# Hyena's weight low parts computed in an earlier stage and kept in HBM, with a fourth load buffer in the hyena stage

## The chip, the cores and the metric

The kernel runs on one core of a Trainium2 chip. The core has five engines that each work through their own list of instructions in order: TensorE (PE, with weight loads shown apart as PEld), VectorE (DVE), ScalarE (ACT), GpSimd (POOL) and SyncE (SP). SP and POOL issue transfers; sixteen DMA engines carry them out. The metric is the device time of one execution in microseconds (us), as the median of several runs; lower is better.

## The reference

One token sequence of 256 rows and 1024 columns goes through three blocks, all in float32: a mixer of stick-breaking attention and memory attention followed by a feed-forward block with a squared relu, then latent attention (MLA) followed by a gated feed-forward block with a short convolution, then a hyena mixer followed by a second such feed-forward block. Every block ends in a layer norm of the scaled input plus the block's result. The two parts that the change touches are

```python
h = jnp.square(jax.nn.relu(x @ w_up[layer]))
x = layer_norm(DN_ALPHA * x + h @ w_down[layer], ...)
...
u = dwconv_centred(x @ w_in, w_short)
v, g1, g2 = jnp.split(u, 3, axis=-1)
z = v
for o, gate in enumerate((g1, g2)):
    k_f = jnp.fft.rfft(two_sided_kernel(filt[:, o, 0], filt[:, o, 1]), n=n, axis=0)
    y = jnp.fft.irfft(jnp.fft.rfft(z, n=n, axis=1) * k_f, n=n, axis=1)[:, :length]
    z = gate * (y + d_bias[o] * z)
return z @ w_o
```

The first is the squared-relu feed-forward (w_up is 1024 x 4096, w_down 4096 x 1024). The second is hyena: an input product with w_in (1024 x 3072), a convolution of width three, then two long convolutions, which the kernel does as products with cosine and sine matrices.

## The kernel before, in words

**Split products.** TensorE takes float32r, a rounded float32. To keep float32's precision every matrix is split into a high part, which is the value rounded by a copy, and a low part, which is the value minus the high part; a product is then three products: high by high, low by high and high by low. `split` (line 66) does it with one ACT copy and one DVE subtraction.

**Weights.** `weights` (line 74) brings a weight tile of 128 x 1024 (512 KB): SP loads it into one of three raw buffers (`wraw`), ACT writes the high part `whi` (line 67), and DVE the low part `wlo` (line 68). High and low parts have five slots each, so a tile's slot is free again when PE has used the tile five earlier. With `dma=True` the low part takes another way: ACT writes the negated high part into `wlo` (lines 84 and 85), and POOL's queue issues a second transfer of the same tile from HBM (high-bandwidth memory) that adds the weight to what lies there (line 86). DVE has no part in it. The raw buffer is free when both ACT copies are done.

**The squared-relu stage** has 32 steps. In step i PE multiplies the tile of w_up five steps ahead (`gemm_wide`, lines 110 to 112), ACT and DVE turn the result into h and split it (`ff1_act`, `act_split`), and PE multiplies the h of step i with a tile of w_down into four accumulator banks (lines 116 to 118). Each step takes two weight tiles. Besides, the rotation tables and the three layers of hyena's filter network are made there.

**The hyena stage** reads the x of the gated feed-forward block before it. Output tiles 0 to 3 of its input product come out of that block's end; tiles 4 to 23 are made by `hy_mm`, three times eight matmuls each into a PSUM bank `hin`. Tiles 0 to 7 are v, 8 to 15 g1 and 16 to 23 g2. `dwconv` runs the short convolution (one ACT pass, two DVE passes); for v and g1 PE then turns the tile over (`hyt`). `v_fin` splits v into `zh` and `zl`: `z0` is the first half of its columns (tiles 0 to 3), `z1` the second (tiles 4 to 7). `spectrum` multiplies z with the forward matrix (`X`) and, on DVE, with the filter's spectrum: four passes of up to 128 x 2048 into `spec_q` and `spec_w`. `even_odd` and `both` split the result into `yh` and `yl`, and `back1` and `back2` multiply that with the inverse matrix (`y`). The first long convolution runs through `back1` for both halves, the second through `back2`. In the end the result is multiplied with `hy_w_o`, eight tiles (`Down`, `acc`), the first four with `dma=True`.

The table `HY_DMA` says which of the tiles 4 to 23 take their low part by the accumulating transfer: eleven of them, 10, 12, 14 and 16 to 23. The main text of the stage (from `z0, z1 = new_z(), new_z()`) gives an order in which things are recorded; a scheduler then sets each engine's order by readiness and priority. `tc.issue_after(...)` keeps what is recorded in its scope behind a named instruction.

## Time and profile before

| | us |
|---|---|
| median of 3 runs | 965.1 (963.51 to 965.26) |
| the profiled execution | 964.65 |
| its span, first to last instruction | 962.9 |
| PE busy | 932.9 (97% of the span) |
| DVE busy | 761.1 (79%) |
| ACT busy | 539.9 (56%) |
| POOL busy | 64.0 (7%) |
| granted TensorE clock, mean | 0.992 |

The rows in fences are as the profile's views print them. A row of the trace in order of time has the start in us from the span's start, the duration, the engine, the line of the kernel, the operation and the tiles as out<-in, and in brackets how long the engine had stood idle before it and what ended that. "L68 DVE wlo<-wraw,whi" is line 68 on DVE writing `wlo` from `wraw` and `whi`. The granted clock is the share of full speed that TensorE was given. The DMA share is the mean busy share of the sixteen DMA engines.

### The profile page before, as it was taken

How to read it: one execution, taken by the hardware profiler on the slowest of the kernel's cores; microseconds unless marked ns; L12 is line 12 of the kernel's file. 1: busy time of each engine (PE TensorE's matmuls, PEld its weight loads, DVE VectorE, ACT ScalarE, POOL GpSimd, SP SyncE). 2: the span in 40 equal slices, each digit the busy share in tenths (PEclk: the TensorE clock that was granted, in tenths of full speed). 3: DMA queues.
4: the chain of work that ended last, by engine and by line, in shares of the span. 5: the costliest groups of instructions: out<-in, count | busy, mean ns of one | idle time of the engine just before them, and what ended most of it. 6: DMA issues, size and time to landing. Idle time of an engine off the chain costs nothing.

```text
span 962.9 us, 15208 instructions
## 1 busy us (share of the span) xinstructions
PE 932.9 (97%) x5808; PEld 823.7 (86%) x5808; DVE 761.1 (79%) x1201; ACT 539.9 (56%) x878; POOL 64.0 (7%) x61
## 2 busy tenths in 40 slices
PE   9999999999999999999999999998989999999996
PEld 6889788888887898788899999888978799999995
DVE  6887679777667879779889788889779878777776
ACT  4676636454445577556666566445675355555551
POOL 0000000000000010011312211001210000000000
PEclk9999999999999999999999999999989999999999
DMA  7764536655665443576555556436995565555551
GB/s 248 261 198 132 166 117 223 204 175 181 192 193 193 160 126 109 176 248 220 184 170 177 176 182 198 153 98 159 262 242 144 173 231 184 181 192 185 186 177 44
DMA packets 51082, 173.83 MB, mean 181 GB/s; under 512 B 6236, under 2 KB 7101, under 8 KB 50881
## 3 DMA queue, kind: packets, MB, share of 16 engines
q1 hardware_dynamic: 48656, 164.34, 52.6%
q0 software_dynamic: 2352, 8.52, 4.6%
q8 instruction: 46, 0.75, 0.3%
q14 instruction: 28, 0.22, 0.1%
HBM read 171.13 MB, written 1.05 MB: 179 GB/s over the span
## 4 chain that ended last, share of the span: by engine, by line
PE 75%; DVE 11%; DMA 7%; ACT 4%; issue 2%; SPq 0%; DVEq 0%; ACTq 0%; POOLq 0%
PE up L102 23%; PE acc L116 9%; PE acc L117 9%; PE acc L118 9%; PE up L110 5%; PE f L199 5%; DVE wlo L68 3%; PE up L112 3%; PE proj L102 2%; DMA wraw<-w_v 1%; ACT whi L67 1%; DMA wraw<-hy_w_in 1%; DMA wraw<-ffn_w_up_f 1%; PE hin L102 1%; DMA wraw<-w_qk 1%
## 5 line engine op out<-in xcount | busy, mean ns | idle before, releaser
L68 DVE TENSOR_TENSOR wlo<-wraw,whi 128x1024 fp32r<-128x1024 f32 (+1 forms) x255 | 310.4, 1220 | 78.4 <-ACT whi L67 77.5
L67 ACT ACTIVATE whi<-wraw 128x1024 fp32r<-128x1024 f32 (+1 forms) x255 | 265.2, 1044 | 128.1 <-PE acc L117 45.8
L102 PE MATMUL up<-x,whi 128*128 128x256 f32 x1280 | 173.7, 283 | 2.0 <-DVE t L790 2.0
L102 PEld LDWEIGHTS up<-x,whi 128*128 128x128 f32 x1280 | 164.8, 191 | 6.2 <-ACT whi L67 2.1
L118 PE MATMUL acc<-wlo,hh 128*128 128x512 f32 x304 | 119.9, 396 | 0.0
L116 PE MATMUL acc<-whi,hh 128*128 128x512 f32 x304 | 119.9, 396 | 0.0
L117 PE MATMUL acc<-whi,hl 128*128 128x512 f32 x304 | 119.9, 395 | 0.0
L102 PE MATMUL up<-x,wlo 128*128 128x256 f32 x640 | 89.8, 283 | 0.0
L787 ACT ACTIVATE t<-up,wc 128x256 f32<-128x256 f32 x80 | 37.7, 473 | 91.8 <-PE up L102 89.0
L102 PEld LDWEIGHTS up<-x,wlo 128*128 128x128 f32 x640 | 82.4, 192 | 0.0
L788 DVE SCALAR_TENSOR_TENSOR t<-up,wc,t 128x255 f32<-128x255 f32 x80 | 38.2, 479 | 46.3 <-ACT t L787 46.0
L118 PEld LDWEIGHTS acc<-wlo,hh 128*128 128x128 f32 x304 | 57.1, 188 | 13.5
L116 PEld LDWEIGHTS acc<-whi,hh 128*128 128x128 f32 x304 | 57.4, 189 | 11.3 <-ACT hh L67 0.5
L117 PEld LDWEIGHTS acc<-whi,hl 128*128 128x128 f32 x304 | 57.0, 188 | 11.0 <-DVE hl L68 0.3
L110 PE MATMUL up<-x,whi 128*128 128x512 f32 x224 | 56.6, 395 | 0.0
L165 POOL TENSOR_TENSOR ln_rs<-ln_rs,mhalf 128x1 f32<-128x1 f32 x12 | 11.5, 958 | 646.3 <-DVE ln_rs L164 646.3
L110 PEld LDWEIGHTS up<-x,whi 128*128 128x128 f32 x224 | 41.8, 188 | 10.6 <-issue 1.1
L102 PE MATMUL hin<-x,whi 128*128 128x256 f32 x320 | 46.7, 292 | 0.0
L102 PEld LDWEIGHTS hin<-x,whi 128*128 128x128 f32 x320 | 42.7, 199 | 0.3
L790 DVE SCALAR_TENSOR_TENSOR t<-up,wc,t 128x255 f32<-128x255 f32 x80 | 38.3, 480 | 2.1
L67 ACT ACTIVATE hh<-h 128x256 fp32r<-128x256 f32 x32 | 13.1, 415 | 39.1 <-DVE h L544 38.0
L112 PEld LDWEIGHTS up<-x,wlo 128*128 128x128 f32 x224 | 30.6, 190 | 2.3
(404 smaller groups left out, 1665.2 us busy)
## 6 DMA issues: line engine op xcount, KB each, us to landing
wraw<-ffn_w_up SPq DMA_DIRECT2D x80, 512.0 KB, 4.2
wraw<-ffn_w_down SPq DMA_DIRECT2D x44, 512.0 KB, 3.7
wraw<-w_down SPq DMA_DIRECT2D x32, 512.0 KB, 3.5
wraw<-w_up SPq DMA_DIRECT2D x28, 512.0 KB, 4.3
wraw<-hy_w_in SPq DMA_DIRECT2D x20, 512.0 KB, 5.1
wraw<-w_qk SPq DMA_DIRECT2D x14, 512.0 KB, 4.5
wlo<-hy_w_in POOLq DMA_DIRECT2D x11, 512.0 KB, 9.4
wraw<-w_out SPq DMA_DIRECT2D x8, 512.0 KB, 3.4
```

The costliest lines, as they stand in the source:

```text
L67: nc.scalar.activation(hi, src, AF.Copy)
L68: nc.vector.tensor_tensor(lo, src, hi.bitcast(F32), op=ALU.subtract)
L102: nc.tensor.matmul(ps, a[:, off + k * P:off + (k + 1) * P], m[:, k, :], start=i == 0, stop=i == len(seq) - 1)
L110: nc.tensor.matmul(ps, wh[:, k * P:(k + 1) * P], xx[:, k], start=k == 0, stop=False)
L112: nc.tensor.matmul(ps[:, :S], wl[:, k * P:(k + 1) * P], xh[:, k, :], start=False, stop=k == KT - 1)
L116: nc.tensor.matmul(ps, ah, mh, start=start, stop=False)
L117: nc.tensor.matmul(ps, al, mh, start=False, stop=False)
L118: nc.tensor.matmul(ps, ah, ml, start=False, stop=stop)
L199: nc.tensor.matmul(ps, x[xi][:, k, tb], ws[k // 2][wi][:, o:o + 512], start=i == 0, stop=i == len(seq) - 1)
L787: norm["act"] = nc.scalar.activation(dst, ps, AF.Copy, scale=w3[:, 1:2])
L788: nc.vector.scalar_tensor_tensor(dst[:, 1:], ps[:, :S - 1], w3[:, 0:1], dst[:, 1:], op0=ALU.mult, op1=ALU.add)
L790: norm["dve"] = nc.vector.scalar_tensor_tensor(dst[:, :S - 1], ps[:, 1:S], w3[:, 2:3], dst[:, :S - 1], op0=ALU.mult, op1=ALU.add)
```

## The change

1. **Low parts ahead of time.** `HY_DMA` shrinks to tiles 20, 21 and 22. For tiles 10 to 19 the low part is made in the squared-relu stage: at every second step from 1 to 21 `low_ahead` has POOL write a small mark that depends on the h made last, and behind it (for the first ten) issue a load of the next tile. Two steps later ACT and DVE split that tile in place, behind the split of the h made last by then, and POOL stores the low part to a tensor in HBM.
2. **Loading them.** In hyena those ten tiles take `low=`: ACT makes the high part alone, and SP loads the low part into its slot. Tile 23 goes back to the split by ACT and DVE.
3. **A fourth raw buffer.** During hyena every fourth `raw_tile` comes from a buffer in that stage's own pool. The room is found there by four buffers for `u` instead of six.
4. **z1 first.** z1's two `v_fin` now stand ahead of the first `spectrum` instead of among the products that follow it.
5. **hy_w_o's copies.** The tiles of `hy_w_o` that are accumulated by transfers are issued only after the first y part of `both`: their ACT copies and transfers are kept behind it.

```diff
-HY_DMA = (10, 12, 14, 16, 17, 18, 19, 20, 21, 22, 23)
+HY_AHEAD = range(10, 20)
+HY_DMA = (20, 21, 22)
...
     def raw_tile():
+        extra["n"] += 1
+        if extra["pool"] is not None and extra["n"] % (RAW_BUFS + 1) == 0:
+            return extra["pool"].tile([P, 1024], F32, name="wraw", tag="wraw_x")
         return wraw.tile([P, 1024], F32, name="wraw", tag="wraw")
...
+        if low is not None:
+            nc.scalar.activation(hi[:, :n], raw[:, :n], AF.Copy)
+            nc.sync.dma_start(lo[:, :n].bitcast(F32), low)
+            return hi, lo
...
+    ahead = {"todo": list(HY_AHEAD), "raw": None}
+
+    def low_ahead(act):
+        marks = [tc.issue_after(i.ins) for i in norm["split"]]
+        if ahead["raw"] is not None:
+            nt, raw = ahead["raw"]
+            hi = p2.tile([P, 1024], F32R, name="la_hi", tag="la_hi")
+            with marks[0], marks[1]:
+                split(hi, raw, raw)
+            lows[nt] = dram.tile([P, 1024], F32, name=f"low{nt}")
+            nc.gpsimd.dma_start(lows[nt], raw)
+            ahead["raw"] = None
+        if ahead["todo"]:
+            nt = ahead["todo"].pop(0)
+            raw = p2.tile([P, 1024], F32, name="la_raw", tag="la_raw", bufs=2)
+            mark = small.tile([P, 1], F32, name="mark", tag="mark")
+            done = nc.gpsimd.tensor_copy(mark, act[1][:, :1].bitcast(F32))
+            with tc.issue_after(done.ins):
+                nc.gpsimd.dma_start(raw, A["hy_w_in"][nt - 4])
+            ahead["raw"] = nt, raw
...
+        if i % 2 and i < 2 * len(HY_AHEAD) + 2:
+            low_ahead(ready[-1])
...
+    extra["pool"] = p4
...
-        w = weights(A["hy_w_in"][nt - 4], dma=nt in HY_DMA)
+        w = weights(A["hy_w_in"][nt - 4], dma=nt in HY_DMA, low=lows.get(nt))
...
-            u = p4.tile([P, S], F32, name="u", tag="u", bufs=6)
+            u = p4.tile([P, S], F32, name="u", tag="u", bufs=4)
...
-    s0 = spectrum(0, 0, z0, True)
-    v_fin(z1, 0, 4, va)
-    ga = pair_mm(8)
-    v_fin(z1, 1, 6, vb)
+    v_fin(z1, 0, 4, va)
+    v_fin(z1, 1, 6, vb)
+    s0 = spectrum(0, 0, z0, True)
+    ga = pair_mm(8)
...
+    yparts = norm["y"]
...
     for k in range(4):
-        dn.add((z0[0][:, k, :], z0[1][:, k, :]), A["hy_w_o"][k], True)
+        with tc.issue_after(yparts[0].ins):
+            dn.add((z0[0][:, k, :], z0[1][:, k, :]), A["hy_w_o"][k], True)
```

How instructions stand after scheduling, at three places (a number, the line, the operation with its tiles, and xN for N alike in a row). SP's list where hyena's weights are loaded; `hy_w_in` are its tiles from number 4 on, `hy_w_in_f` and `wc` belong to the stage's beginning and the one before. Before:

```order
170 L82 DMA wraw<-hy_w_in_f 128x1024 x3
171 L873 DMA wc<-ffn_w_conv 128x132
172 L82 DMA wraw<-hy_w_in_f 128x1024
173 L82 DMA wraw<-hy_w_in 128x1024 x20
174 L82 DMA wraw<-hy_w_o 128x1024 x8
```

The same place now; `low_1878` and the like are the stored low parts, from tile 10 on:

```order
173 L91 DMA wraw<-hy_w_in 128x1024 x8
174 L94 DMA wlo<-low_1878 128x1024
175 L91 DMA wraw<-hy_w_in 128x1024
176 L94 DMA wlo<-low_1985 128x1024
177 L91 DMA wraw<-hy_w_in 128x1024
178 L94 DMA wlo<-low_2117 128x1024
179 L91 DMA wraw<-hy_w_in 128x1024 x3
180 L94 DMA wlo<-low_2224 128x1024
181 L91 DMA wraw<-hy_w_in 128x1024
182 L94 DMA wlo<-low_2346 128x1024
```

The ten low loads stand among the raw loads in one list, so each waits for those ahead of it; on POOL's list eleven accumulating transfers of hyena's tiles have become three.

DVE's list around the first `spectrum` (its passes are `spec_w` and `spec_q`; `hyt_7019` before holds tiles 4 and 5 turned over, `hyt_7081` and `hyt_7096` now hold tiles 4 and 5, and 6 and 7). Before:

```order
737 L947 TENSOR_TENSOR zl<-hyt_6943,zh 128x2x256
738 L788 SCALAR_TENSOR_TENSOR u<-hin,ws,u 128x255
739 L68 TENSOR_TENSOR wlo<-wraw,whi 128x1024
740 L790 SCALAR_TENSOR_TENSOR u<-hin,ws,u 128x255
741 L68 TENSOR_TENSOR wlo<-wraw,whi 128x1024
742 L976 TENSOR_TENSOR spec_w<-ev,X_6995 128x512 x2
743 L976 TENSOR_TENSOR spec_w<-ev,X_7007 128x512 x2
744 L68 TENSOR_TENSOR zl<-hyt_7019,zh 128x2x256
745 L978 TENSOR_TENSOR spec_q<-spec_w,Kf 128x2048
746 L788 SCALAR_TENSOR_TENSOR u<-hin,ws,u 128x255
747 L979 TENSOR_TENSOR spec_q<-spec_q 128x2x512
748 L980 TENSOR_TENSOR spec_w<-spec_w,Kf 128x2048
```

And now:

```order
751 L986 TENSOR_TENSOR zl<-hyt_7035,zh 128x2x256
752 L828 SCALAR_TENSOR_TENSOR u<-hin,ws,u 128x255
753 L826 SCALAR_TENSOR_TENSOR u<-hin,ws,u 128x255 x2
754 L828 SCALAR_TENSOR_TENSOR u<-hin,ws,u 128x255
755 L71 TENSOR_TENSOR zl<-hyt_7081,zh 128x2x256
756 L828 SCALAR_TENSOR_TENSOR u<-hin,ws,u 128x255
757 L1015 TENSOR_TENSOR spec_w<-ev,X_7117 128x512 x2
758 L71 TENSOR_TENSOR zl<-hyt_7096,zh 128x2x256
759 L826 SCALAR_TENSOR_TENSOR u<-hin,ws,u 128x255
760 L1015 TENSOR_TENSOR spec_w<-ev,X_7129 128x512 x2
761 L828 SCALAR_TENSOR_TENSOR u<-hin,ws,u 128x255
762 L1017 TENSOR_TENSOR spec_q<-spec_w,Kf 128x2048
```

Both halves of z1 are now finished ahead of the long passes, and the two weight low parts that stood here (tiles 8 and 9) have moved up, ahead of z0's end.

ACT's list around the last but one y, that of the second convolution's first half (`yh`; `g_6820` and `g_6912` are g2, `zh<-u` the result of `back2`). Before:

```order
558 L85 ACTIVATE wlo<-wraw 128x1024
559 L787 ACTIVATE g_6820<-hin,ws 128x256
560 L84 ACTIVATE whi<-wraw 128x1024
561 L67 ACTIVATE yh<-spec_q 128x512 x2
562 L85 ACTIVATE wlo<-wraw 128x1024
563 L787 ACTIVATE g_6820<-hin,ws 128x256
564 L84 ACTIVATE whi<-wraw 128x1024
565 L67 ACTIVATE yh<-spec_w 128x512 x2
566 L787 ACTIVATE g_6820<-hin,ws 128x256
```

And now:

```order
561 L70 ACTIVATE yh<-spec_q 128x512 x2
562 L825 ACTIVATE g_6912<-hin,ws 128x256
563 L70 ACTIVATE yh<-spec_w 128x512 x2
564 L825 ACTIVATE g_6912<-hin,ws 128x256
565 L97 ACTIVATE whi<-wraw 128x1024
566 L98 ACTIVATE wlo<-wraw 128x1024
567 L97 ACTIVATE whi<-wraw 128x1024
568 L98 ACTIVATE wlo<-wraw 128x1024
569 L70 ACTIVATE zh<-u 128x256
570 L97 ACTIVATE whi<-wraw 128x1024
```

The copies of `hy_w_o` (whi by L97, wlo by L98) that stood among y's parts and before them now all stand behind them, and the third and fourth of them among the parts of `back2`.

More of the change, by code (lines that the diff above doesn't have):

```diff
@@ L50, in block_kernel @@
     wspl = ctx.enter_context(tc.tile_pool(name="wspl", bufs=SPLIT_BUFS))
+    dram = ctx.enter_context(tc.tile_pool(name="dram", bufs=1, space=bass.MemoryType.DRAM))
+    lows = {}
     lnp = ctx.enter_context(tc.tile_pool(name="lnp", bufs=1))
@@ L66, in split, with weights @@
     def split(hi, lo, src):
-        nc.scalar.activation(hi, src, AF.Copy)
-        nc.vector.tensor_tensor(lo, src, hi.bitcast(F32), op=ALU.subtract)
+        return (nc.scalar.activation(hi, src, AF.Copy),
+                nc.vector.tensor_tensor(lo, src, hi.bitcast(F32), op=ALU.subtract))
     norm = {"inst": None, "after": 0}
+    extra = {"pool": None, "n": 0}
     def raw_tile():
+        extra["n"] += 1
+        if extra["pool"] is not None and extra["n"] % (RAW_BUFS + 1) == 0:
+            return extra["pool"].tile([P, 1024], F32, name="wraw", tag="wraw_x")
         return wraw.tile([P, 1024], F32, name="wraw", tag="wraw")
-    def weights(ap, dst=None, dma=False):
+    def weights(ap, dst=None, dma=False, low=None):
         n = ap.shape[-1]
@@ L299, in act_split @@
         lo = pool.tile([P, S], F32R, name=tag + "l", tag=tag + "l", bufs=bufs)
-        split(hi, lo, ps)
+        norm["split"] = split(hi, lo, ps)
         return hi, lo
@@ L1011, in both @@
                 for j, t in enumerate((q, w)):
-                    split(y[0][:, i, j], y[1][:, i, j], t[:, i, 0])
+                    norm["y"] = split(y[0][:, i, j], y[1][:, i, j], t[:, i, 0])
         return y
@@ L1040, in back2 @@
                     n == 0, n == 3)
-            t = p4.tile([P, S], F32, name="u", tag="u", bufs=6)
+            t = p4.tile([P, S], F32, name="u", tag="u", bufs=4)
             nc.vector.tensor_tensor(t, ps[:, :S], g2[:, 4 * c + q, :], op=ALU.mult)
@@ L1092, in block_kernel @@
     x, utok = dn.end(gb, ALPHA_2, A["ffn_w_up_f"][1], [(room[:, i, 0], room[:, i, 1]) for i in range(4)])
+    extra["pool"] = None
     ph.close()
```

## The prediction

> **What bounds the kernel now.** I read the page first, then a table of stretches, then the rows in order of time around each wait of TensorE, and last the DMA queues of two stages.
>
> ```profile
> PE 932.9 (97%) x5808; PEld 823.7 (86%) x5808; DVE 761.1 (79%) x1201; ACT 539.9 (56%) x878; POOL 64.0 (7%) x61
> ```
>
> TensorE (PE) is busy 97% of the span, so all that an edit can win is its 30 us of idle time and what the clock withholds. The stretches that matter, in us from the span's start (columns: length, then busy time and count by engine, granted clock, DMA share, GB/s):
>
> ```profile
> 633.00:763.00 130.00, 120.66 (x788) 109.71 (x787) 110.70 (x164) 77.66 (x112) 14.11 (x16) 0.96 0.72 195
> 650.00:676.40 26.40, 22.37 (x166) 21.66 (x165) 23.43 (x34) 13.25 (x21) 2.68 (x3) 0.94 0.64 169
> 676.40:706.40 30.00, 25.56 (x177) 23.50 (x175) 21.08 (x31) 22.94 (x33) 6.07 (x7) 0.94 1.03 260
> 706.40:724.60 18.20, 18.20 (x119) 16.85 (x120) 16.03 (x22) 14.09 (x21) 4.37 (x5) 0.91 0.98 233
> 724.60:763.00 38.40, 37.52 (x205) 31.38 (x204) 35.02 (x54) 17.45 (x27) 0.99 (x1) 1.00 0.59 183
> 656.00:664.00 8.00, 5.44 (x33) 5.24 (x33) 7.30 (x10) 2.37 (x4) 0.88 (x1) 0.79 0.38 85
> 698.00:712.00 14.00, 10.01 (x39) 7.97 (x38) 7.71 (x15) 10.55 (x16) 2.62 (x3) 0.76 1.04 261
> 150.00:265.00 115.00, 115.00 (x571) 95.15 (x570) 86.24 (x151) 60.84 (x94) 0.00 (x0) 1.00 0.60 187
> 420.00:440.00 20.00, 18.18 (x140) 17.36 (x139) 17.18 (x27) 14.21 (x24) 4.39 (x3) 1.00 0.84 289
> ```
>
> Hyena's input product and convolutions fill 633 to 763. There PE idles 130.00 - 120.66 = 9.3 us, and its clock loses (1 - 0.79) x 8 = 1.7 us at 656 to 664 and (1 - 0.76) x 14 = 3.4 us at 698 to 712. Together 14.4 us: the ceiling of a gain in this stage. The squared-relu stage (150 to 265 of it) has PE at 115.00 of 115.00: nothing to win, only to lose. The rows of PE in hyena that waited long (start, duration, line, operation, and in brackets the idle time before it with its releaser):
>
> ```profile
> 659.14 0.50 PE L935 MATMUL hyt<-ident,u 128*128 128x128 f32 x2 [2.56 <-DVE u L790]
> ...
> 670.01 1.22 PE L102 MATMUL hin<-x,wlo 128*128 128x256 f32 x8 [1.47 <-DMA wlo<-hy_w_in]
> ...
> 700.10 1.54 PE L102 MATMUL hin<-x,wlo 128*128 128x256 f32 x8 [1.82 <-DMA wlo<-hy_w_in]
> ...
> 706.38 0.47 PE L116 MATMUL y<-yh,c_inv1h 128*128 128x512 f32 x1 [2.17 <-DVE g L790]
> ```
>
> Three causes: a convolution on DVE (VectorE) queued behind the spectrum's long products (2.56 us); low parts that an accumulating DMA of the POOL queue brings late (1.47, 1.82); and the y product at 706.38 (2.17), late because its inputs were. Those go back to ACT (ScalarE) and a raw load, in ACT's rows
>
> ```profile
> 699.67 1.06 ACT L85 ACTIVATE wlo<-wraw 128x1024 fp32r<-128x1024 f32 x1 [2.69 <-DMA wraw<-hy_w_in]
> ```
>
> and DVE's:
>
> ```profile
> 702.12 0.69 DVE L68 TENSOR_TENSOR yl<-spec_q,yh 128x512 fp32r<-128x512 f32 x1 [6.93 <-ACT yh L67]
> ```
>
> ACT stood 2.69 us for a raw tile, and DVE 6.93 us for the copies of y that ACT has behind it. The load was slow because the 16 DMA engines were full: share 1.03 in 676 to 706. By queue and by issue, 633 to 724 (q0 is POOL's, q1 SP's; the last figure is the median landing in us):
>
> ```profile
> q0 software_dynamic: 1919, 7.01, 40.7%
> q1 hardware_dynamic: 3024, 11.01, 36.5%
> ...
> wraw<-hy_w_in SPq DMA_DIRECT2D x16, 512.0 KB, 5.1
> wlo<-hy_w_in POOLq DMA_DIRECT2D x11, 512.0 KB, 9.4
> wraw<-hy_w_o SPq DMA_DIRECT2D x7, 512.0 KB, 8.4
> wlo<-hy_w_o POOLq DMA_DIRECT2D x4, 512.0 KB, 8.6
> ```
>
> 40.7% of 91 us is 37.0 us for 7.01 MB: 2.77 us of all 16 engines for an accumulation of 512 KB (0.524 MB). 36.5%, 33.2 us for 11.01 MB, makes 1.58 us for a plain load.
>
> **The change, part by part.** *Hyena's transfers.* Eight accumulations go (22.2 us of the engines), ten plain loads of low parts come (15.8 us): 70.2 us becomes 63.8. ACT loses eight negating copies (8 x 1.06, the 699.67 row, = 8.5 us), and a raw buffer is free again after one copy. A low load can start when the low slot of the tile five earlier has been read, five tiles of PE's work ahead of its use, and a tile is three times the eight matmuls of the 670.01 row (1.22), about 3 us with overlap; raw loads land in 5.1. I expect PE to wait for none. SP holds them in line with the raw loads, so a low load that waits for its slot holds up raw loads behind it, and the reverse; the fourth raw buffer covers that. Cover gone, each late tile costs like today's, 1.5 to 1.8 us.
>
> [...]
>
> *The first y product (stretch 650 to 676.4).* DVE's chain sets when it can start; two of its rows:
>
> ```profile
> 660.52 1.22 DVE L68 TENSOR_TENSOR wlo<-wraw,whi 128x1024 fp32r<-128x1024 f32 x1
> ...
> 669.70 1.29 DVE L68 TENSOR_TENSOR yl<-spec_w,yh 128x512 fp32r<-128x512 f32 x2
> ```
>
> Today y's last low part ends at 669.70 + 1.29 = 671.0, but PE, delayed, only comes at 676.4. The change takes tile 11's low part (1.22, the first row) off this chain, and puts the low parts of tiles 8 and 9 and z1's finish ahead of the spectrum, so that no transpose waits behind the long products: y's parts are there by about 669.8. PE, without its waits (26.40 - 22.37 = 4.0) and the half clock (1.7), comes at 670.7, 0.9 us after them. Gain 5.7; late next is this same chain.
>
> *The second (676.4 to 706.4).* Idle 30.00 - 25.56 = 4.4, and half of the 3.4 us of clock, 1.7: PE comes at 694.6 in the new time, 670.7 + 30.0 - 6.1. Without DVE's 6.93 us wait y's parts could be there that much before today's 706.4, at 699.5; shifted by 5.7 that is 693.8, 0.8 ahead of PE. Gain 6.1.
>
> *The third (706.4 to 724.6)* has no idle time, but the other 1.7 us of half clock, which follows the 2.17 us gap. Gain 1.7. Tile 23's low part comes back to DVE here (1.22), where DVE is busy 16.03 of 18.20; tiles 13 and 15 give as much back before. Convolution buffers fall from six to four: a convolution then waits for the transposes of the one four before, done a pair of tiles earlier, so nothing; with that cover gone, some tenths at each. Sum of the gains: 13.5 us.
>
> *hy_w_o's copies behind y's parts.* Four raw tiles are copied twice by ACT and accumulated into by POOL. Today the last of those DMAs is issued at 722.72 in POOL's rows,
>
> ```profile
> 722.72 0.88 POOL L86 DMA_DIRECT2D wlo<-hy_w_o  x1 [2.44 <-ACT wlo L85]
> ```
>
> before the second half's y product and 11 us before the first product with hy_w_o, in PE's rows:
>
> ```profile
> 724.57 0.28 PE L116 MATMUL y<-c_inv2h,yh 128*128 128x256 f32 x1
> ...
> 733.97 0.40 PE L116 MATMUL acc<-whi,zh 128*128 128x512 f32 x1
> ```
>
> Behind the change the first pair of copies (2.1 us) starts about when that y product does (724.57 here) and POOL issues 0.5 later; with a landing of 8.6 that is 11.2 us in. PE wants the low part 733.97 + 0.5 - 724.57 = 9.9 in. Late by 1.3 at the median landing, by 0 if the copies get ahead of the order that I read, by 2.1 at 9.4, the median of hyena's own tiles. I take 1.0, just under the nearest row's.
>
> *The squared-relu stage.* Ten times in about 115 us come a load and a store of 512 KB on POOL's queue, one more split on ACT and DVE, and a mark on POOL that holds the load back. The page's rows for such a split, the stage's DMA (150 to 305) and ACT's largest wait for a weight slot there:
>
> ```profile
> L68 DVE TENSOR_TENSOR wlo<-wraw,whi 128x1024 fp32r<-128x1024 f32 (+1 forms) x255 | 310.4, 1220 | 78.4 <-ACT whi L67 77.5
> L67 ACT ACTIVATE whi<-wraw 128x1024 fp32r<-128x1024 f32 (+1 forms) x255 | 265.2, 1044 | 128.1 <-PE acc L117 45.8
> ```
> ```profile
> q1 hardware_dynamic: 8615, 29.14, 60.1%
> ...
> wraw<-w_down SPq DMA_DIRECT2D x28, 512.0 KB, 3.4
> wraw<-w_up SPq DMA_DIRECT2D x22, 512.0 KB, 4.3
> ```
> ```profile
> ACT whi L67 <- PE up L110: 22.6, 21, 1.9
> ```
>
> DVE goes from 86.2 to 98.4 of 115 us, ACT from 60.8 to 71.2: both keep room. A transfer is 60.1% of 155 us over 29.14 MB, 1.68 us; twenty make 33.6, so the share rises from 0.60 to 0.89. A store from POOL's queue isn't in this trace; I price it as a load, and with 2.77, the accumulation's, as its dear end the share is 0.99. PE uses a weight tile every 2.82 us (571 matmuls in 115 us, 28 for two tiles). Three raw buffers, each taken for its landing, the two copies (1.04, 1.22) and some tenths, 2.6 us in all beside the landing, keep that pace up to a landing of 3 x 2.82 - 2.6 = 5.9 us. Medians are 3.4 and 4.3; a transfer of POOL's delays what it overlaps by about its own 1.68, so I estimate 5. ACT mostly waits for PE to free a slot (22.6 us), so weights stand ready. On POOL nothing but the layer norm's powers comes behind these transfers, eleven steps after the last. Price 0 to 6, taken 0.5 since the estimate is under the limit; below nothing is excluded, as PE is full there.
>
> *New short waits* at the y products, with 0.9 us of room at the first: 0 to 5, taken 1.0, near today's smallest (1.47).
>
> Net: 13.5 - 1.0 - 0.5 - 1.0 = 11.0 us. The profiled execution took 964.65 (span 962.9 and 1.75 around it), 0.45 below the median of the runs, 965.1. So 954.1, rounded to 954.0.
>
> **The rivals.** *The gaps move and the clock stays low.* DVE's chain is 2 us later than I sum at two of the y products. Gaps of about 1.3 us each return, and a half-clock stretch (1.7) follows one: 4.3 lost, 958.4. For it: DVE is busy 23.43 of 26.40. Against: it loses work there. [...]
>
> *The DMA engines stay the bound: no change.* If a low load among raw ones costs what an accumulation did, the stretches with a share near 1 stay as they are; only the 2.56 us gap goes with its half clock (4.3), less the 2.5 of costs and 0 to 3.2 for two more transfers: 963 to 966. Against: 1.58 against 2.77. [...]
>
> *Slower: the squared-relu stage starves.* hy_w_o's raw loads landed in 8.4 us where the engines were full. At 8.4 a raw buffer turns in 11.0 us, a tile each 3.67, 0.85 over the pace; 41 tiles make 35 us, less four split tiles of backlog (11.3): 23.5 lost, 977. It decides from a landing of about 7.5, where the loss (22.4 - 11.3 = 11.1) eats the net gain. For it: share 0.89 to 0.99. Against: 420 to 440 moves 289 GB/s at 0.84, and the mark paces POOL by PE's own progress. The case: 967 to 977.
>
> **How the numbers follow.** Forecast 0.63 (951 to 957), moved gaps 0.20 (957 to 962), DMA-bound 0.07 (963 to 966), starved 0.10 (967 to 977). A measurement of this kernel can tell about 0.2%, 1.9 us. Faster 0.63 + 0.20 = 0.83, same 0.07, slower 0.10. The low end, 950.5, is the whole ceiling of 14.4 us; the range up to 963 leaves out the last two cases and a little below.
>
> **What would show it.** Right: 150 to 265 with PE full, DMA share near 0.9, landings near 5; no wait of PE for hyena's low parts; clock 1.00 from 650 to 720; the first two y products near 671 and 695; a wait of about 1 us before the first products with hy_w_o. Wrong: PE waiting in the squared-relu stage, landings over 6 there, or y products where they stand today.

## The result, and the profile after

| | before | changed |
|---|---|---|
| median of 4 runs, us | 964.65 (963.51 to 965.26) | 956.53 (955.58 to 959.44) |
| ratio to before, 95% interval | | 0.9922 (0.9898 to 0.9946) |
| profiled execution: time, span | 964.65, 962.9 | 956.31, 954.0 |
| granted clock, mean | 0.992 | 0.997 |

The changed kernel is faster by 8.1 us in the medians and by 8.9 in the spans of the two profiled executions, where the net forecast was 11.0. A later set of twelve runs of the same kernel ("changed again" below) has a median of 959.7, at 0.9946 of the kernel before: 5 us faster. First the page's row for PE (TensorE), then the table of stretches of the changed kernel, columns as before the change:

```profile
PE 928.3 (97%) x5808; PEld 820.7 (86%) x5808; DVE 768.8 (81%) x1209; ACT 540.3 (57%) x880; POOL 72.6 (8%) x83
```
```profile
150.00:265.00 115.00, 115.00 (x572) 95.37 (x571) 95.08 (x159) 67.94 (x101) 13.17 (x29) 1.00 0.80 264
656.00:664.00 8.00, 8.00 (x67) 7.91 (x66) 7.76 (x8) 3.99 (x6) 0.00 (x0) 1.00 0.80 259
698.00:712.00 14.00, 14.00 (x108) 13.53 (x107) 13.70 (x16) 5.02 (x10) 0.00 (x0) 1.00 0.11 40
722.00:740.00 18.00, 14.09 (x64) 10.49 (x64) 14.43 (x15) 9.12 (x12) 0.86 (x1) 1.00 0.97 279
```

The squared-relu stage still has PE full (115.00 of 115.00). The two stretches that had PE idle and a clock of 0.79 and 0.76 are full at 1.00. From 698 to 712 the DMA engines are nearly idle (0.11); from 722 to 740 they are full (0.97), and PE has 3.9 us of idle time that was not there before. PE's rows show where:

```profile
672.34 0.48 PE L129 MATMUL y<-yh,c_inv1h 128*128 128x512 f32 x1
...
695.23 0.39 PE L129 MATMUL y<-yh,c_inv1h 128*128 128x512 f32 x1
...
712.62 0.35 PE L129 MATMUL y<-c_inv2h,yh 128*128 128x256 f32 x1 [0.23 <-DVE g L828]
...
722.05 0.39 PE L129 MATMUL acc<-whi,zh 128*128 128x512 f32 x1
...
724.34 0.50 PE L131 MATMUL acc<-wlo,zh 128*128 128x512 f32 x1 [1.66 <-DMA wlo<-hy_w_o]
...
728.13 0.50 PE L131 MATMUL acc<-wlo,zh 128*128 128x512 f32 x1 [0.73 <-DMA wlo<-hy_w_o]
...
731.98 0.50 PE L131 MATMUL acc<-wlo,zh 128*128 128x512 f32 x1 [0.78 <-DMA wlo<-hy_w_o]
...
735.79 0.51 PE L131 MATMUL acc<-wlo,zh 128*128 128x512 f32 x1 [0.74 <-DMA wlo<-hy_w_o]
...
738.23 0.28 PE L129 MATMUL y<-c_inv2h,yh 128*128 128x256 f32 x1
```

and, of the kernel before, the first y product and the one behind hy_w_o's four tiles:

```profile
676.44 0.48 PE L116 MATMUL y<-yh,c_inv1h 128*128 128x512 f32 x1
...
745.18 0.29 PE L116 MATMUL y<-c_inv2h,yh 128*128 128x256 f32 x1
```

The first two y products come at 672.3 and 695.2 (676.4 and 706.4 before), and no hyena product waits for a low part. But each of the first four tiles of hy_w_o waits for its own accumulated low part. From the first product with hy_w_o to the next y product it takes 738.23 - 722.05 = 16.2 us; before, 745.18 - 733.97 = 11.2. The 5.0 us lost are more than the 3.9 of idle time: the first product behind a gap takes 0.50 to 0.51 instead of 0.39 to 0.40, and its overlap with the one ahead of it (0.16: products otherwise start 0.23 to 0.24 apart) is gone.

To compare kernels I cut the way from the hyena stage's first transposes (f4t) to the next stage's first product (up) at the same products in each trace. This keeps out what happens ahead of f4t, which differs by up to 3.5 us between two executions of the same kernel (626.49 and 630.02 for the changed one). y1, y2 and y3 are the first products of the first three y in PE's rows. The products with X stand in other stretches from kernel to kernel (0.23 us each; 7 of them between y1 and y2 in the changed kernel, 12 in that with low parts ahead alone), so a single column is good to 1 or 2 us between kernels; the sums don't have this.

| kernel | f4t to y1 | y1 to y2 | y2 to y3 | y3 to hy_w_o | its four tiles | then to up | sum | ratio of times to before (95%) |
|---|---|---|---|---|---|---|---|---|
| before | 50.70 | 29.94 | 18.19 | 9.40 | 11.21 | 32.10 | 151.5 | |
| changed | 45.85 | 22.89 | 17.39 | 9.43 | 16.18 | 30.38 | 142.1 | 0.9922 (0.9898 to 0.9946) |
| changed again | 45.95 | 22.89 | 17.38 | 9.44 | 15.25 | 30.37 | 141.3 | 0.9946 (0.9923 to 0.9969) |
| no hold | 46.87 | 22.89 | 17.38 | 9.45 | 11.20 | 31.37 | 139.2 | 0.9906 (0.9882 to 0.9929) |
| no hold again | 45.84 | 22.89 | 17.38 | 9.44 | 11.20 | 31.34 | 138.1 | 0.9888 (0.9867 to 0.9910) |
| hy_w_o split plainly | 47.22 | 22.89 | 17.39 | 9.44 | 11.19 | 32.84 | 141.0 | 0.9914 (0.9898 to 0.9931) |
| three buffers | 48.08 | 23.16 | 16.06 | 10.16 | 16.60 | 33.55 | 147.6 | 0.9991 (0.9978 to 1.0005) |
| three buffers, no hold | 47.11 | 23.16 | 16.07 | 13.12 | 11.20 | 31.78 | 142.4 | 0.9952 (0.9933 to 0.9971) |
| z1 late | 45.57 | 23.57 | 16.95 | 9.25 | 16.52 | 30.38 | 142.2 | 0.9930 (0.9915 to 0.9946) |
| no low parts ahead | 50.02 | 30.10 | 15.14 | 10.13 | 16.19 | 31.59 | 153.2 | 0.9996 (0.9980 to 1.0011) |
| low parts ahead alone | 51.24 | 23.80 | 17.06 | 9.05 | 11.20 | 32.70 | 145.1 | 0.9965 (0.9944 to 0.9987) |
| low loads by POOL | 45.81 | 22.90 | 17.38 | 9.45 | 16.63 | 30.73 | 142.9 | 0.9940 (0.9915 to 0.9964) |
| hy_w_o ahead too | 45.77 | 22.89 | 17.38 | 9.44 | 11.20 | 30.93 | 137.6 | 0.9973 (0.9956 to 0.9990) |
| twice the traffic | 47.14 | 22.89 | 17.38 | 9.44 | 16.32 | 30.37 | 143.5 | 1.0150 (1.0127 to 1.0173) |

The column f4t to y1 needs a word. In the traces of four kernels (hy_w_o split plainly, three buffers with the hold, no low parts ahead, low parts ahead alone) a stretch at half clock (granted 0.50), worth 1.7 us, stands right behind f4t. The other traces have the same gap of 1.1 us there and no such stretch. I take it for a chance of the execution (last section); it is taken off below where I say so.

### The profile page after: what moved, and what is told of

Read it like the earlier page. It is cut to its first block, busy times and chain, and to the rows that moved or that the text cites. A ratio compares the mean times of both kernels' runs of the same rounds, so it can differ in the third digit from the quotient of the medians.

```text
span 954.0 us, 15307 instructions
## 1 busy us (share of the span) xinstructions
PE 928.3 (97%) x5808; PEld 820.7 (86%) x5808; DVE 768.8 (81%) x1209; ACT 540.3 (57%) x880; POOL 72.6 (8%) x83
## 4 chain that ended last, share of the span: by engine, by line
PE 81%; DVE 7%; DMA 6%; ACT 4%; issue 2%; DVEq 0%; SPq 0%; ACTq 0%
PE up L115 23%; PE acc L129 9%; PE acc L131 9%; PE acc L130 9%; PE up L123 5%; PE f L212 5%; PE hin L115 5%; PE up L125 3%; PE proj L115 2%; DVE wlo L71 2%; ACT whi L70 1%; DMA wlo<-hy_w_o 1%; DMA wraw<-w_qk 1%; DMA wraw<-w_v 1%; PE ln_t L191 1%
## 5 line engine op out<-in xcount | busy, mean ns | idle before, releaser
L70 ACT ACTIVATE whi<-wraw 128x1024 fp32r<-128x1024 f32 (+1 forms) x253 | 262.4, 1044 | 117.1 <-PE acc L130 46.1
L115 PE MATMUL hin<-x,whi 128*128 128x256 f32 x320 | 44.7, 286 | 0.0
L70 ACT ACTIVATE hh<-h 128x256 fp32r<-128x256 f32 x32 | 13.1, 413 | 36.9 <-DVE h L557 35.8
```

The costliest lines, as they stand in the source:

```text
L70: return (nc.scalar.activation(hi, src, AF.Copy), nc.vector.tensor_tensor(lo, src, hi.bitcast(F32), op=ALU.subtract))
L115: nc.tensor.matmul(ps, a[:, off + k * P:off + (k + 1) * P], m[:, k, :], start=i == 0, stop=i == len(seq) - 1)
```

## The experiments

**No hold (twice).** Part 5 undone:

```diff
-        with tc.issue_after(yparts[0].ins):
-            dn.add((z0[0][:, k, :], z0[1][:, k, :]), A["hy_w_o"][k], True)
+        dn.add((z0[0][:, k, :], z0[1][:, k, :]), A["hy_w_o"][k], True)
```

> Part 5 undone: hy_w_o's copies and accumulations are no longer kept behind y's parts; the rest is the changed kernel. In the changed kernel TensorE waits four times for hy_w_o's accumulated low parts (1.66, 0.73, 0.78 and 0.74 us, 3.9 in all; the four tiles of products take 16.2 us from first to next y product where they took 11.2 before: 5.0 lost). Theory: this is where the missing gain went. Undone, the four waits go, but eight copies of 1.04 us stand between 697 and 712, where ScalarE is busy about 11 of 17 us, so y's parts and the y product at 712.6 come 1 to 3 us later: 952.5 to 955, 1.5 to 4 below the changed kernel's 956.5. Rival A: the hold earns more than it costs; the copies push the y product back by 5 us or more: 957 or above. Rival B: the waits for hy_w_o are due to the engines being full in that stretch (DMA share 0.96 in 724 to 740) whenever the copies are made; then they stay near 3.9 and the time is 956 to 957.

> Part 5 undone once more, on the chip of the next three, so that the medians can be set side by side. Theory: from the hyena stage's first transposes (f4t) to the next stage's first product it takes 139 to 140 us, against 141.3 and 142.1 in the two profiles of the changed kernel and 151.5 before; the first product with hy_w_o follows the y product by 9.4 us and the four tiles take 11.2: a ratio of 0.989 to 0.992 to the kernel before. Rival: the first profile was lucky, the waits for hy_w_o's low parts come back in part: 142 and a ratio above 0.992.

Measured: 955.53 us (952.95 to 960.44) and 955.27 (952.13 to 958.45). POOL's rows show the four accumulations, first in the changed kernel, then without the hold:

```profile
715.21 0.86 POOL L99 DMA_DIRECT2D wlo<-hy_w_o  x1 [24.77 <-ACT wlo L98]
717.10 0.86 POOL L99 DMA_DIRECT2D wlo<-hy_w_o  x1 [1.04 <-ACT wlo L98]
719.61 0.86 POOL L99 DMA_DIRECT2D wlo<-hy_w_o  x1 [1.65 <-PE y L131]
722.61 0.86 POOL L99 DMA_DIRECT2D wlo<-hy_w_o  x1 [2.14 <-ACT wlo L98]
```
```profile
700.82 0.86 POOL L99 DMA_DIRECT2D wlo<-hy_w_o  x1 [8.99 <-ACT wlo L98]
705.58 0.86 POOL L99 DMA_DIRECT2D wlo<-hy_w_o  x1 [3.89 <-ACT wlo L98]
708.46 0.86 POOL L99 DMA_DIRECT2D wlo<-hy_w_o  x1 [2.02 <-ACT wlo L98]
711.76 0.86 POOL L99 DMA_DIRECT2D wlo<-hy_w_o  x1 [2.45 <-ACT wlo L98]
```

Held back, they start 7 us ahead of the first product, all four within 7.4 us, and land in 11.7 (median). Free, they go out from 700.8, in the very stretch in which the engines otherwise idle, and land in 8.3, all ahead of that product at 723.5. The four waits are gone (11.20 against 16.18). And the y product that the hold was to guard doesn't move: y2 to y3 is 17.38 both ways. The expectation had it 1 to 3 us later and ScalarE (ACT) busy for 11 of 17 us there; in the changed kernel ACT is busy 6.55 of 17.4 us between those two y products (695.2 to 712.6), so the copies fit into its gaps. Of the 5.0 us 1.0 is given back behind (31.4 against 30.4, in part by short waits of PE at the last tiles and the layer norm, 0.19 and 0.30 us). The hold therefore costs 2 to 4 us here and earns nothing that these runs show. In the medians the two pairs say it less sharply: 0.9906 against 0.9922 is within the intervals, 0.9888 against 0.9946 is not. These ratios are each to the kernel before in the same set of runs; no set has both kernels. Taking off what the clock withheld in each run, (1 - granted clock) x span, leaves a median of 950.8 us for the twelve runs without the hold and 953.9 for the sixteen with it: 3.1 apart, as the traces say.

**hy_w_o split plainly.** `True` left out in the same call, the hold kept.

> The first four tiles of hy_w_o take their low part from VectorE (a plain split) instead of the accumulating transfer; the hold behind y's parts stays. Four accumulations and four negating copies go, four subtractions of 1.22 us come to VectorE, which is busy 12.6 of 16 us from 724 to 740 and 11.6 of 14 from 710 to 724. Theory (the accumulations in a row are the cost): the four waits go, of the 5.0 us at least 3 come back: 952 to 953.5. Rival (the raw loads on full engines are the cost, they land in 10.5 us): the waits move to the high parts, 955.5 to 957. Rival (VectorE becomes the bound): the subtractions stand ahead of the multiplications behind the y product, and z's parts come late by up to 4.9: 954 to 957.

Measured: 956.26 us (955.60 to 958.41). The waits go as without the hold (11.19), so it is the accumulations, not the raw loads, that came late. Of the 5.0 us 2.5 are given back before the next stage (32.84 against 30.38), where VectorE (DVE) has four subtractions of 1.22 us more ahead of the layer norm; one wait of PE for DVE there is 0.53, and the rest is not traced further. With the half clock behind f4t taken off, the sum is 139.3. The theory's time (952 to 953.5) was missed, since less than 3 us of the 5.0 stayed gained. Of the two rivals, the raw loads fell and VectorE has part of the truth.

**Three buffers, with and without the hold.** Part 3 undone, and in the second kernel part 5 too:

```diff
-    extra["pool"] = p4
...
-            u = p4.tile([P, S], F32, name="u", tag="u", bufs=4)
+            u = p4.tile([P, S], F32, name="u", tag="u", bufs=6)
```

> Part 3 undone: three raw buffers in hyena, six for u; the rest is the changed kernel. Theory of the prediction: the fourth buffer covers raw and low loads that hold each other up in SP's one list; without it some tiles come late, each at 1.5 to 1.8 us as before the change, and one such gap brings a stretch at half clock (1.7): two to four tiles late, 960 to 965. Rival: raw loads landing in 4.8 us at a tile every three are covered by three buffers as well, and the time is the changed kernel's, 956 to 957.

> Three raw buffers and no hold; z1 first and the low parts ahead stay. It tells whether the 5.5 us that the fourth buffer was worth (f4t to next product 147.6 with three buffers, 142.1 with four) is due to SP's one list or to the hold, which keeps hy_w_o's raw tiles in the buffers. Theory 1 (the hold): 141 to 143, a ratio near 0.992. Theory 2 (SP's list): 145 to 147.6, a ratio of 0.996 to 0.999.

Measured: 964.80 us (962.30 to 967.52), nearly the whole gain gone, and 961.21 (959.27 to 963.90). SP's rows (its queue of loads) from 630 us on, with four buffers and with three:

```profile
629.82 9.11 SPq L91 DMA_DIRECT2D wraw<-hy_w_in  x4
640.61 0.33 SPq L94 DMA_DIRECT2D wlo<-low  x1
```
```profile
639.81 17.01 SPq L91 DMA_DIRECT2D wraw<-hy_w_in  x6
656.88 3.96 SPq L94 DMA_DIRECT2D wlo<-low  x5
```

The first low load leaves 16 us later, behind raw loads that wait for a buffer. That lateness alone costs little: from the first y product to the third PE has no idle time with three buffers either (23.16 and 16.06). The loss stands later. With the hold, ACT waits 10.0 us in all for raw tiles of hy_w_o (0 and 6.9 in the two profiles of the changed kernel), and the last stretch is 3.2 us longer (33.55 against 30.38). In ACT's rows with three buffers and no hold, a raw tile of hy_w_o comes late with y's parts next in the list:

```profile
716.51 1.06 ACT L70 ACTIVATE whi<-wraw 128x1024 fp32r<-128x1024 f32 x1 [0.79 <-DMA wraw<-hy_w_o]
717.47 1.13 ACT L70 ACTIVATE yh<-spec_w 128x512 fp32r<-128x512 f32 x2
```

There PE waits 2.58 us in the y product, up to 718.14, and a stretch at half clock follows (0.50 from 719.14 to 721.14, 1.70 us lost with its edges): the 13.12 of the table. Without the hold the fourth buffer is worth 142.4 - 138.1 or 139.2, 3.2 to 4.3 us; with it 147.6 less 1.7 of half clock against 141.3 to 142.1, 3.8 to 4.6. So theory 1 of the second kernel fell, though its sum (141 to 143) was met and its ratio (near 0.992) was not: the sum is lower because the hold's own cost is gone, not because the buffer is worth less. The two costs add up: 2 to 4 us for the hold, 3.2 to 4.6 for the missing buffer. The first kernel's time (960 to 965) was met too, but not by hyena tiles that come late, as its theory had it: one product waits 0.3 us for a low load.

**z1 late.** Part 4 undone: the two `v_fin(z1, ...)` stand behind `spectrum` and `pair_mm(8)` again.

> Part 4 undone: z1's two finishes back among the products behind the spectrum's recording; the rest is the changed kernel. Theory: the wait of 2.56 us for a convolution of u behind the spectrum's long passes and its half clock (1.7) come back, since the long passes and not the low parts make that wait: the first y product at about 676 instead of 672.3, 960 to 961. Rival: VectorE, relieved of low parts, has room, and the wait stays under 1 us: 956.5 to 957.5.

Measured: 958.64 us (957.08 to 959.48). The wait of 2.56 us does not come back; f4t to y1 is 45.57 against 45.85. The rival's mechanism holds; its time (956.5 to 957.5) was missed. That the median lies 2 us above the changed kernel's isn't from this part: the sum is the same, 142.2 and 142.1. One wait for hy_w_o was 2.0 us long there, with half clock behind it (0.50 from 726.81 to 728.81, 1.71 us lost with its edges).

**No low parts ahead.** Parts 1 and 2 undone (and `low_ahead` not called), 3 to 5 kept:

```diff
-HY_AHEAD = range(10, 20)
-HY_DMA = (20, 21, 22)
+HY_AHEAD = range(0)
+HY_DMA = (10, 12, 14, 16, 17, 18, 19, 20, 21, 22, 23)
```

> Parts 1 and 2 undone: no low part is made ahead, and the eleven tiles 10, 12, 14 and 16 to 23 take theirs by the accumulating transfer as before; the fourth buffer, z1 first and the hold of hy_w_o's copies stay. Theory of the prediction (the accumulations fill the engines, 2.77 us for 512 KB against 1.58): the DMA share stays near 1 from y1 to y2, the stretch between the first two y products takes 27 to 30 us as before instead of 22.9, TensorE waits for low parts again: 960 to 965. Rival (the fourth raw buffer alone makes the gain, since without it the run gave 964.8): the stretch takes 23 to 24 us and the time is 956 to 958.

Measured: 964.63 us (962.55 to 967.39), no gain. PE's rows between the first two y products:

```profile
682.83 1.21 PE L115 MATMUL hin<-x,wlo 128*128 128x256 f32 x8 [1.32 <-DMA wlo<-hy_w_in]
...
689.30 0.74 PE L974 MATMUL hyt<-ident,u 128*128 128x128 f32 x4 [1.43 <-ACT ev L1013]
...
695.21 1.21 PE L115 MATMUL hin<-x,wlo 128*128 128x256 f32 x8 [1.35 <-DMA wlo<-hy_w_in]
```

y1 to y2 takes 30.10, as before the change (29.94), against 22.89, at a DMA share of 0.95. Two shorter waits for low parts (0.77 and 0.43) come on top, so 3.9 us of the 5.3 idle are for low parts and 1.4 for ACT. The theory holds: the fourth buffer does not make this gain. Its worth without low parts ahead isn't measured here, since the hold's cost (16.19 at hy_w_o's tiles) is in this kernel too. Nor do the runs part what the DMA engines gain from what ACT gains, which has eight copies fewer in the changed kernel.

**Low parts ahead alone.** Parts 1 and 2 on the kernel before.

> Parts 1 and 2 alone on the kernel before: low parts made ahead and loaded, but three raw buffers, z1 at its old place and no hold of hy_w_o's copies. Theory 1 (low parts and fourth buffer only pay together: with three buffers SP's one list makes raw loads wait behind low loads and the reverse): 964 to 967, as the run with three buffers (964.8), with some us either way for z1 (2) and the hold (1 to 5). Theory 2 (the loss with three buffers came from its meeting with the hold, which has hy_w_o's raw tiles keep the buffers until 712): 959 to 961.

Measured: 961.21 us (958.31 to 967.96), just above theory 2's span and below theory 1's; the runs with three buffers above say that the hold was half of the matter. y1 to y2 is 23.80, so that gain needs parts 1 and 2 alone. But the wait of PE behind the spectrum's long passes is there, longer than before the change:

```profile
665.55 0.70 PE L973 MATMUL hyt<-ident,u 128*128 128x128 f32 x2 [4.63 <-DVE u L828]
```

So z1 first removes a wait with three buffers, and none with four. The times don't show it: the kernel with three buffers, z1 first and no hold also takes 961.21, and loses at the third y what it wins here.

**Low loads by POOL.** In `weights`, `nc.sync.dma_start(lo, low)` becomes `nc.gpsimd.dma_start(lo, low)`, beside an unedited run of the changed kernel on the same chip.

> The changed kernel itself, unedited, beside the next three on one chip, so that they can be set against it directly. Expected: 956 to 957 by its runs so far, 8 to 9 below the kernel before.

> The ten stored low parts come by POOL's queue instead of SP's; still plain loads, the rest is the changed kernel. It prices the queue apart from the kind of transfer. Theory (the kind counts): a plain load of 512 KB takes the sixteen engines about 1.6 to 1.8 us from POOL's queue too, the stretches of hyena stay as they are, and the time is 956 to 957.5; raw loads may even start sooner, since no low load stands between them. Rival (the queue counts, 2.77 us for whatever POOL issues): ten loads cost 12 us more of the engines, the share comes near 1 between the first two y products, and TensorE waits there again: 959 to 963. [...]

Measured: 958.78 us (957.51 to 962.00), the changed kernel 959.70 (955.94 to 967.80), both above what was expected, and by these ranges the same. No product waits for a low load in either. The queues from 640 to 705, in the changed kernel (first profile) and with POOL's queue:

```profile
q1 hardware_dynamic: 3975, 14.45, 62.1%
q0 software_dynamic: 432, 1.57, 13.3%
...
wlo<-low SPq DMA_DIRECT2D x10, 512.0 KB, 3.5
```
```profile
q0 software_dynamic: 1872, 6.82, 35.5%
...
wlo<-low POOLq DMA_DIRECT2D x10, 512.0 KB, 5.8
```

In the changed kernel q0 holds three accumulations: 13.3% of 65 us, 8.65 us, or 2.88 each; SP's plain loads take 62.1% of 65 us over 14.45 MB, 1.47 for 512 KB. With POOL's queue q0 has ten plain loads more: 23.1 us less 8.65 leaves 1.44 each. The kind of transfer makes the difference here (from POOL's queue 2.88 for an accumulation, 1.44 for a plain load), not the queue (1.47 for a plain load from SP's); what the queue changes is the time to landing (5.8 against 3.5), for which nothing had to wait here.

**hy_w_o ahead too.** `low_ahead` also makes hy_w_o's first four tiles, so it runs to step 29; no hold:

```diff
-        if i % 2 and i < 2 * len(HY_AHEAD) + 2:
+        if i % 2 and i < 2 * N_AHEAD + 2:
...
-            dn.add((z0[0][:, k, :], z0[1][:, k, :]), A["hy_w_o"][k], True)
+        dn.add((z0[0][:, k, :], z0[1][:, k, :]), A["hy_w_o"][k], False, lows["o%d" % k])
```

> A candidate to beat both: hy_w_o's first four low parts are made ahead in the squared-relu stage too (fourteen tiles instead of ten, at steps 1 to 29), loaded by SP, and no hold. Four accumulations (2.77 us of the engines each) and four negating copies (1.04) go from hyena, four plain loads (1.6) come; eight more transfers come to the end of the squared-relu stage. Theory: nothing in hyena waits for hy_w_o, f4t to next product 138 to 139.5, at most 1 better than without the hold: ratio 0.988 to 0.991. Rival: splits and transfers up to two steps before the end of the squared-relu stage push its layer norm or the next stage's weights back by 1 to 3 us, and the time is above the run without the hold.

Measured: 963.01 us (960.86 to 967.51). In hyena it has the lowest sum of all (137.6), and it loses that many times over at the end of the squared-relu stage: the next stage's first product (f with f4h) comes at 324.8, against 313.4 to 316.6 in the ten traces with ten tiles. ACT's rows there:

```profile
309.89 1.06 ACT L71 ACTIVATE f4h<-wraw 128x1024 fp32r<-128x1024 f32 x1 [0.22 <-DMA wraw<-mla_w_in_f]
313.20 1.06 ACT L71 ACTIVATE la_hi<-la_raw 128x1024 fp32r<-128x1024 f32 x1 [2.25 <-DMA la_raw<-hy_w_o]
315.72 1.06 ACT L71 ACTIVATE f4h<-wraw 128x1024 fp32r<-128x1024 f32 x1 [1.46 <-DMA wraw<-mla_w_in_f]
```

and PE's:

```profile
307.87 0.79 PE L130 MATMUL acc<-whi,hh 128*128 128x512 f32 x1 [2.77 <-ACT whi L71]
...
323.09 1.60 PE L192 MATMUL ln_t<-ident,xt 128*128 128x128 f32 x8 [2.91 <-DVE xt L184]
```

The copy of the last low part waits 2.25 us for its load and stands in ACT's list ahead of the next stage's weights, whose raw buffers therefore stay taken; DVE's subtraction stands ahead of the layer norm; and half clock stands at two gaps of 2.8 and 2.9 us (granted 0.50; 3.4 us lost at the first, 1.7 at the second). (The first gap ends with a weight's copy at 306.78, which stands behind the copy of another low part, 1.06 us from 305.81.) The rival named the mechanism, and put 1 to 3 us on it where 8 to 11 were lost.

**Twice the traffic.** Each load and store in `low_ahead` issued a second time.

> In the squared-relu stage every load and every store of the ten tiles is issued twice (the second load into a tile that nobody reads, the second store into a second tensor): forty transfers on POOL's queue instead of twenty, the rest is the changed kernel. It tries the rival that the stage starves. In the changed kernel the DMA share there is 0.80 and twenty transfers are 26.5% of 115 us, so forty ask for 1.06. Theory (the engines are shared by all queues; weights fall behind once landings pass 5.9 us, and a loss shows from about 7.5): landings of 6 to 9 us, TensorE waits for weights, 150 to 265 stretches by 3 to 12 us: 960 to 969. Rival (POOL's transfers give way, since a mark holds each load back until TensorE has got on, and only the low parts come later): landings under 6, no wait, 956 to 958.

Measured: 979.99 us (978.99 to 983.08). The stage's table row (150 to 265) and landings (150 to 305), then the landings of the changed kernel:

```profile
150.00:265.00 115.00, 110.76 (x540) 89.24 (x539) 82.96 (x144) 58.28 (x88) 22.03 (x39) 1.00 0.82 285
```
```profile
wraw<-w_up SPq DMA_DIRECT2D x23, 512.0 KB, 8.1
wraw<-w_down SPq DMA_DIRECT2D x23, 512.0 KB, 7.5
```
```profile
q0 software_dynamic: 2880, 10.49, 21.3%
...
wraw<-w_down SPq DMA_DIRECT2D x28, 512.0 KB, 4.8
wraw<-w_up SPq DMA_DIRECT2D x23, 512.0 KB, 4.6
```

The stage starves as that rival of the prediction says: the next stage starts at 336.5 instead of 313.4 and 316.6 in the two profiles of the changed kernel, 20 to 23 us late. With forty transfers on POOL's queue instead of twenty, SP's loads land in 8.1 (w_up) and 7.5 us (w_down) instead of 4.6 and 4.8: POOL's transfers slow SP's, as the theory's shared engines would have it. PE waits 12.0 us for high and low parts of weights there. The ring of three buffers at a landing of 7.8 gives 41 x ((7.8 + 2.6) / 3 - 2.82) - 11.3 = 15 us by the prediction's formula, low by a quarter to a third. The formula has no term for the clock: three stretches at half clock (0.50) stand ahead of the next stage (269.3, 300.0 and 323.9), 5.1 us together, which make up most of the difference. The DMA share hardly tells the two apart (0.82 against 0.80); the landing does.

## Why the prediction was right, point by point

It was right on the sign and near on the size: 954.0 forecast, 956.5 measured, 950.5 to 963 given. How near is in part luck: the later twelve runs have 959.7, and two of them lie above 963. Against the two profiled executions (8.9 us):

| term | forecast | measured | from |
|---|---|---|---|
| A, first y product | 5.7 | 4.9 | f4t to y1, 50.70 to 45.85 |
| B, second | 6.1 | 7.1 | y1 to y2, 29.94 to 22.89 |
| C, third stretch's clock | 1.7 | 0.8 | y2 to y3, 18.19 to 17.39 |
| hy_w_o's copies late | -1.0 | -5.0 | its four tiles, 11.21 to 16.18 |
| behind them | 0 | 1.7 | to the next stage, 32.10 to 30.38 |
| squared-relu stage | -0.5 | within the spread | first f at 313.4 to 316.6 in ten traces with ten tiles; 314.3 before, 314.4 without low parts ahead |
| new short waits | -1.0 | none at y1 and y2; 0.98 ahead of y1 and 0.23 at y3 are inside A and C | 0.56 and 0.42 at 642.8 and 649.5; 712.62 |
| before f4t, and after up | 0 | -0.75 and 0.2 | 625.74 to 626.49; 185.62 to 185.39 |

- **A, B and C** sum to 12.8 of 13.5. The new short waits stand ahead of y1 and make most of what A lacks. Two products with X have moved behind y2 (10 there before, 12 now), so B is larger and C smaller by 0.5 us, which is a gain of neither. That the ten low parts bring B is shown by the run without them, which has all other parts and takes 30.10. For A the step "z1's finish ahead of the spectrum, so that no transpose waits" was the wrong reason: z1 late costs nothing with four buffers.
- **The fourth buffer** stood in the prediction as a cover, at 1.5 to 1.8 us for each late tile. It is worth 3.2 to 4.6 us, and without it the whole change measures as none (0.9991). The step had the wrong place: without it PE hardly waits for hyena's tiles (0.3 us), but hy_w_o's raw tiles and what stands behind them in ACT's list come late.
- **hy_w_o's copies** are the mis-sized term. The step that failed is "Late by 1.3 at the median landing": it asked only when the first tile is there. The 1.66 us of idle time at that tile is near it (POOL issued at 715.21, 0.30 us behind the copy's end, where the step had 0.5). But the landing it used (8.6) was for accumulations issued over 13.2 us (709.56 to 722.72); held together behind y's parts, four go out within 7.4 us on full engines (0.97), and landings grow from 9.1 to 13.1 (median 11.7). They come 3.8 us apart, as the four rows of PE show, where a tile's products take 2.8 (a fourth of 11.2), so each tile in turn is late, by 0.73 to 0.78 of idle time more. The first tile had been priced, and the step took it for all four. The end of the range (2.1) was too low for the same reason. I also took for granted that something is gained by the hold; the runs without it show no y product that moves.
- **Behind them**, 1.7 us came back: the likely reason is that DVE and the next weights get ahead while PE stands. That the run without the hold gets 1.0 less there fits this for 1.0 of the 1.7; the rest is open.
- **The squared-relu stage**: PE full, landings 4.8 and 4.6 for an estimate of 5, a share of 0.80 for 0.89. The price of a transfer, stores included, was right (21.3% of 155 us over 10.49 MB is 1.65 us for 512 KB, 1.68 used). The share is lower since the weights' own transfers, which the prediction left as they were, took 53.1% of 150 to 265 instead of 59.5%. The step "weights stand ready" no longer holds, though PE lost nothing clear of the spread by it: from 150 to 305 ACT's waits for weight loads rose from 2.6 to 17.0 us, and its waits for PE to free a slot fell from 29.8 to 7.3. The two runs that load the stage harder show that the cliff is real, and that its place depends on where the transfers stand: four tiles more, up to two steps before its end, cost 8 to 11 us.
- **The rivals.** Moved gaps: gaps did come back, though at hy_w_o and not at y; the clock stayed at 1.00 in this execution (722 to 740) and was 0.50 behind a gap of 2.0 us at the same place in that with z1 late. Engines stay the bound (its 0 to 3.2 us are up to two plain loads of 1.58): y1 to y2 stays as before (30.10) in the run that keeps the accumulations, but not in the changed kernel (22.89). Starved: shown possible with doubled traffic, not met here.

By the traces and the times without the clock's loss, the change without its part 5 is the faster one: 0.9888 (0.9867 to 0.9910) and 0.9906 (0.9882 to 0.9929) of the kernel before.

## What to carry to other kernels

Price a row of late transfers for each of its users, with the landing that they have when they are issued together (here a median of 11.7 us, where 8.6 was taken), and not for the first user alone. A hold that is to protect one engine's list should be tried without it: look first whether that engine has gaps in which the work would fit, and whether the transfers that hang on it have an idle stretch to go in. Work that is moved into an earlier stage must have its loads landed before an in-order engine comes to it; near a stage's end, where the next stage's weights and a layer norm stand behind it, one late load can cost several times its own wait (2.25 us of wait, 8 to 11 lost here, with other waits in it).

## What was not expected of the hardware

Behind the same gap the clock is at half in one execution and not in another. Two rows of PE, with the stretch around each, of the changed kernel and of that with POOL's queue:

```profile
440.27 1.19 PE L115 MATMUL up<-x,whi 128*128 128x256 f32 x8 [2.45 <-DVE t L828]
```
```profile
439.00:445.00 6.00, 4.73 (x32) 4.44 (x33) 6.00 (x9) 2.81 (x7) 3.53 (x2) 1.00 0.38 112
```
```profile
440.91 2.05 PE L115 MATMUL up<-x,whi 128*128 128x256 f32 x8 [2.45 <-DVE t L828]
```
```profile
439.00:445.00 6.00, 4.09 (x22) 4.12 (x23) 6.00 (x10) 2.83 (x6) 3.50 (x2) 0.72 0.33 119
```

Both waited 2.45 us; the clock was 1.00 in the one and 0.72 in the other (0.50 in each us from 440.91 to 443.91), (1 - 0.72) x 6 = 1.7 us. Over the fourteen traces of this study, 24 of 34 idle times of PE of 1.8 us or more had a stretch at half clock within 5 us, and 2 of 30 between 1.3 and 1.8; those 2 are in the starved stage, with other gaps close by. The length of one gap is not the whole of it: behind f4t, where PE idles 0.69 and 1.1 us within 2 us, 4 of the fourteen traces have such a stretch too. In rows of 1 us, summed over nine traces, the loss is 1.69 to 1.71 us in each of 21 stretches, behind gaps of 1.1 us as of 4.63; one loses twice that, 3.41, at the gap of 2.77 us in hy_w_o ahead too. The prediction counted the three such stretches of hyena in its one trace as sure gains (5.1 us); by these counts such a gap pays it some seven times in ten. It also explains much of the spread between executions of one kernel: the sixteen runs of the changed one take 955.6 to 967.8, at granted clocks of 0.997 and 0.989 at the two ends, and 950.8 to 957.2 without the clock's loss. Why such a gap is followed by half clock in one execution and not in another, these runs do not show.
